# Delta rule on one Trainium2 core: key transposes and M v issued ahead of the triangular inverse, T on M v moved into the recursion, one product table parked in DRAM

## The chip, the cores and the metric

The kernel runs on one core of one Trainium2 chip. The metric is the device time of one execution in microseconds; the time of a kernel is the median of its runs.

## The reference, cut to what matters

Two blocks follow each other on x (256 tokens of width 1024, f32). The first has two hybrid layers, each closed by a feed-forward part (relu, squared). The second joins a differential attention and a delta-rule recursion in two directions, and ends with a mixture of small experts. The change touches the recursion alone:

```python
def wkv_scan(s0, scan_in):
    def step(s, inp):
        w, kk, a, k, v, r = inp
        sa = jnp.einsum('dbhij,dbhj->dbhi', s, kk)
        s = s * w[..., None, :] - sa[..., :, None] * (kk * a)[..., None, :] + v[..., :, None] * k[..., None, :]
        return s, jnp.einsum('dbhij,dbhj->dbhi', s, r)
    return lax.scan(step, s0, scan_in)
...
    s_ctx, y_c = wkv_scan(s0, scan_c)
    _, y_x = wkv_scan(s_ctx, scan_x)
    o_bx = rwkv_post(from_scan(y_x), *aux_x, rw_g_up, rw_r_k, rw_ln_g, rw_ln_b)
```

The scan runs over 256 tokens of the context ("ctx") and then, from the state it leaves, over the 256 tokens of x, with 16 heads of 64 in each of two directions. Of ctx only the last state is used. `rwkv_post` is a mean and a variance per head, a bonus term and a gate.

## The kernel before, in words

Products are f32 made of two parts each, so one linear layer is three matmuls per tile (L333 to L335 with 256 columns, called linA here, and L351 to L353, linB). ACT takes a weight's high part (L312, `wh`), DVE the rest (L277, `wl`).

The recursion is done in chunks of 32 tokens: 8 chunks, which are 8 steps n. The heads are split into two halves `hf` of 8. Thus `wkv_front` and `wkv_back` run four times: ctx's first heads inside the feed-forward part of the first layer, ctx's second heads inside that of the second layer, and x's first and second heads (called x0 and x1) in `second`, beside the projections and the attention. The state goes from ctx to x through DRAM (`Sd`, L906, L1632).

`wkv_front` (L1175) prepares a half's chunks. It loads k, v (and r for x), normalises the keys (L1197, L1206), transposes v and parks it in DRAM (`vtd`), builds the decays and the scaled keys KB and WR, and multiplies them (L1299, "PQ products"); DVE masks the result (L271) into the strictly triangular ML and, for x, the causal products NK. L1314 transposes ML's first half, and `din` carries it through DRAM into Bt. Then comes the inverse T of a unit triangular matrix, 31 pairs of DVE instructions with a width that grows to 256 and falls again (L1328 to L1331, a multiplication by L271 and a subtraction by L277), and back through `dout` with a transpose on DVE (L1338). After it stand in the program: the loads of v (UV) and the transposes of the keys (KT, L1353) and of WR (AT, L1363 for x, L1366 for ctx); M v and then T on M v (one loop over `half`, L1383: 8 calls of 32 matmuls of 32x64 for each half, brought back to UV's rows by ACT, L268); T on W (L1395, called W products) and its scaling by DVE (L271, L1403).

`wkv_back` (L1410) is the recursion. In each step n TensorE multiplies the state (L1429, 32 matmuls, called S>U), DVE adds it to T on M v (L1431, two instructions), TensorE makes the update of the state (L1451, 32 matmuls, K>S) and DVE adds it to the decayed state (L274), which GpSimd made (L1436). For x ACT also copies the step's output out of the bank (L1442, four copies). Each step waits for the one before it. For x a tail follows: NK times U (L1471), mean and variance on DVE (L1476, L1482), the scaling, transposes, the gate (L1497, L1498), ACT (L1501) and the store into `od`.

The instructions' order on each engine is made when the kernel is built: a scheduler runs through the program on modelled times and takes what is ready, with `high_priority(offset=30000)` in favour of the recursion's parts. Buffers decide with it: `w4` and `w8` are pools of 5 and 6 buffers in the feed-forward parts, 8 and 9 in `second`, and a tile waits until its buffer's last reader is done. x1's WR lies in the work tiles `hh` and `hl`, in which the attention's output is written as well, so that this output waits for x1's last S>U. The banks for ctx's products come from two pools in turn (`bank`, L220, stream "c").

The attention over x has 16 iterations, each with two exponentials on ACT (L1533), sums on DVE (L1528), a combination (L1539) and matmuls (L1527, L1550). `od` feeds `merge2`, which follows the recursion of x1.

Of the kernel before, what the change touches and what calls it, by code (L numbers as in the profile page):

```python
# [194 lines left out]
class Kern:  # L195
# [22 lines left out]
        return pool.tile(shape, dtype, tag=tag, name=self.uid(tag), **kw)  # L218

    def bank(self):  # L220
        if self.single == "c":
            self.turn += 1
            return self.t(*((self.psm, [128, 512], "m"), (self.psx, [128, 512], "x"))[self.turn % 2])
        if self.single:
            return self.t(self.psm, [128, 512], "m")
        if not self.sfx and self.spare_bank:
            self.turn += 1
            if self.turn % 3 == 0:
                return self.t(self.psx, [128, 512], "x")
        return self.t(self.psr if self.sfx == "r" else self.psw if self.sfx else self.psa, [128, 512], "a")  # L230
# [657 lines left out]
    def ffn(self, l, pool):  # L888

        nc = self.nc  # L890
        hh = self.t(self.work, [128, 8, T], "hh", F32R)
        hl = self.t(self.work, [128, 8, T], "hl", F32R)
        self.normT(self.halves(self.x), self.P["g_ffn"], hh, hl, spare="t")
        self.mods_units(5, self.last)
        self.spare_bank = False
        if l == 0:
            self.ctx_proj(pool)
        with self.stream("n", "c"), self.tc.high_priority(offset=30000):
            self.n4, self.n8 = 5, 6
            tg = self.t(pool, [128, D], "TG", bufs=4)  # L900
            self.wkv_consts(pool, tg[:, T:T + 264])
            wa = tg[:, :T]
            nc.sync.dma_start(wa, self.wad)
            S = self.t(pool, [128, 2, 4, 64], "S")
            self.wkv_back(pool, self.wkv_front(pool, 0, l, self.zc, wa), S)
            nc.sync.dma_start(self.Sd[l], S)  # L906
        with self.stream("t"):
            pw = [self.bank_pair(), [self.score_bank(), self.score_bank()]]
        prev = None
        for i in range(17):  # L910
            cur = None
# [263 lines left out]
    def wkv_front(self, pool, src, hf, zd, wa, own=False):  # L1175


        nc, C, P = self.nc, self.C, self.P2
# [112 lines left out]
        for q in range(4):  # L1291
# [8 lines left out]
            for b in range(2):  # L1300
                for d in range(2):
                    self.mul(ML[:, d, q, b], pq[b][:, d, :, src], strict[:, 1 - d].unsqueeze(1).to_broadcast([128, 4, 32]))
                    if src:
                        self.mul(NK[:, d, q, b], pq[b][:, d, :, 0], incl[:, d].unsqueeze(1).to_broadcast([128, 4, 32]))

        if src:
            for d in range(2):
# [11 lines left out]
            nc.sync.dma_start(din[c, 0].rearrange("k r s -> r k s"), MT.rearrange("p (k s) -> p k s", s=32)[u])  # L1319
        Bt = self.w4(pool, [128, 32, 32])  # L1320
        nc.sync.dma_start(Bt, din.rearrange("c d k r s -> (c d k) r s"))
        X = self.w4(pool, [128, 32, 32])
        nc.gpsimd.memset(X, 0.0)
        nc.vector.memset(X.rearrange("p a b -> p (a b)")[:, 0::33], -1.0)
# [9 lines left out]
        for c in range(2):  # L1334
# [5 lines left out]
        KT = [k.rearrange("p m (q c) x s -> p m q (c x s)", c=2) for k in KB]  # L1340
        UV = [self.w8(pool, [128, 4, 4, 128]) for e in range(2)]
        for g in range(4):
            rows, at = slice(64 * (g % 2), 64 * (g % 2) + 32), slice(32 * g, 32 * g + 32)
            for t in range(2):
                for d in range(2):
                    n = 4 * t + g if d == 0 else 7 - 4 * t - g
                    nc.sync.dma_start(UV[n % 2][rows, n // 2].rearrange("p m c -> p (m c)"), vtd[at, t])
        for q in range(4):
            for d in range(2):
                qd = q if d == 0 else 3 - q  # L1350
                ps = self.bank().rearrange("p (m c) -> p m c", m=4)
                for m in range(4):
                    nc.tensor.transpose(ps[:, m], KT[d][:, m, qd], self.ident)  # L1353
                self.evac(KT[d][:, :, qd], ps)

        AT = [[self.w4(pool, [128, 2, 4, 128]) for h in range(2)] for d in range(2)]
        for q in range(4):
            for d in range(2):
                at = AT[d][q // 2][:, q % 2]
                ps = self.bank().rearrange("p (m c) -> p m c", m=4)  # L1360
                for m in range(4):
                    if src:
                        nc.tensor.transpose(ps[:, m], WR[d][:, m, 2 * q:2 * q + 2].rearrange("p c x s -> p (c x s)"), self.ident)  # L1363
                        continue
                    for c2 in range(2):
                        mm(ps[64 * c2 + 32:64 * c2 + 64, m], WR[d][:, m, 2 * q + c2, 0], self.ident, start=True, stop=True)  # L1366
                if src:
                    self.evac(at, ps)
                else:
                    for c2 in range(2):  # L1370
                        u = slice(64 * c2 + 32, 64 * c2 + 64)
                        self.evac(at[u], ps[u])
        steps = lambda n: [(d, *divmod(n if d == 0 else 7 - n, 2)) for d in range(2)]
        for half in (0, 32):

            for n in range(8):
                uv = UV[n % 2][:, n // 2]
                ps = self.bank().rearrange("p (m b i) -> p m b i", m=4, b=2)
                for m in range(4):
                    for b in range(2):  # L1380
                        for d, q, c2 in steps(n):
                            R = slice(64 * c2 + half, 64 * c2 + half + 32)
                            mm(ps[64 * c2 + 32:64 * c2 + 64, m, b], ML[R, d, q, b, m], uv[R, m, 64 * b:64 * b + 64], start=True, stop=True)  # L1383
                for c2 in range(2):
                    u = slice(64 * c2 + 32, 64 * c2 + 64)
                    self.evac(uv[u], ps[u].rearrange("p m b i -> p m (b i)"))

        for d in range(2):
            pa = [self.bank().rearrange("p (q m s) -> p q m s", q=4, m=4) for c2 in range(2)]
# [6 lines left out]
            for c2 in range(2):  # L1396
# [6 lines left out]
                    nc.vector.tensor_copy(al[:, first // 2], pa[c2][:, first // 2])  # L1403
                old = PC[:, d, :, 2 * lo + c2 + 2 * d - 1:2 * hi + c2 + 2 * d - 2:2].rearrange("p m q -> p q m")
                self.mul(al[:, lo:hi], pa[c2][:, lo:hi], old.unsqueeze(3).to_broadcast([128, hi - lo, 4, 32]))
        Y = [self.w4(pool, [128, 2, 4, 128]) for d in range(2)] if src else None
        W = [w.rearrange("p m c x s -> p (m c x s)") for w in WR] if src else wc.rearrange("p d m c s -> p (d m c s)")
        return src, hf, PC, W, KT, UV, NK, Y, bond if src else None

    def wkv_back(self, pool, state, S, od=None):  # L1410

        src, hf, PC, W, KT, UV, NK, Y, bond = state
        nc, P = self.nc, self.P2
        mm = nc.tensor.matmul
        m0 = 4 * hf
        U64 = [UV[n % 2][:, n // 2].rearrange("p m (b i) -> p m b i", b=2) for n in range(8)]
        for n in range(8):
            dc = [(d, *divmod(n if d == 0 else 7 - n, 2)) for d in range(2)]
            if src or n:
# [26 lines left out]
            for b in range(2):  # L1446
                Q = slice(64 * b, 64 * b + 64)
                for m in range(4):
                    for d, q, c2 in dc:
                        R = slice(64 * c2, 64 * c2 + 64)  # L1450
                        mm(pk[d][Q, m], KT[d][R, m, q, Q], U64[n][R, m, b], start=True, stop=True)  # L1451
            for d in range(2):
                if n or src:
                    self.add(S[:, d], D[:, d] if n else S[:, d], pk[d])
# [2 lines left out]
        if not src:  # L1457
            for d in range(2):
                self.mul(S[:, d], S[:, d], PC[:, d, :, 7 - 7 * d].unsqueeze(2).to_broadcast([128, 4, 64]))
            return  # L1460

        yf = Y[0]
        for t in range(2):
            ps = self.bank().rearrange("p (m b i) -> p m b i", m=4, b=2)
# [543 lines left out]
```

## Time and profile before

| what | us |
|---|---|
| median of 3 runs | 2866.26 |
| lowest and highest of them | 2864.38 and 2883.52 |
| the profiled execution's own time | 2874.03 |
| its span, first to last instruction | 2872.2 |
| TensorE busy in it | 2672.7 (93%) |
| DVE busy, ACT busy | 1945.2 (68%), 1447.4 (50%) |
| mean granted TensorE clock | 0.949 of 2.4 GHz |

Starts are given in us from the first instruction of the profiled execution. A granted clock of 1.00 in a stretch is 2.4 GHz throughout, 0.50 is 1.2 GHz throughout; between them part of the stretch had the one and part the other. A wait is the idle time of an engine just before an instruction, with the name of what ended it. ctx's first heads lie at 395 to 690, its second heads at 1037 to 1301, x0 at 1397 to 1713 and x1 at 1612 to 1867.

### The profile page before, as it was taken

The page shows a single profiled execution, that of the slowest core. Times are in us where ns is not written, and L with a number is a line of the kernel's source. Part 1 is how long each engine was busy: PE and PEld are TensorE (multiplying, and loading weights), DVE is VectorE, ACT ScalarE, POOL GpSimd, SP SyncE. Part 2 cuts the span into 40 slices and gives each one's busy share as a digit, 9 for nine tenths or more (in the row PEclk, how much of TensorE's full clock was granted, in tenths as well). Part 3 has the DMA queues.
Part 4 walks back from the last instruction along what each step waited for, and adds up shares of the span by engine and source line. Part 5 has one row for each costly group of instructions (what it writes and reads, how often), then busy time and mean ns, then how long its engine had stood idle before and what let it go on. Part 6 is the DMA issues. An engine that isn't in the chain of part 4 may idle for free. (4 is left out here: it accounts for less than half of the span.)

```text
span 2872.2 us, 57632 instructions
## 1 busy us (share of the span) xinstructions
PE 2672.7 (93%) x23136; PEld 2344.7 (82%) x23136; DVE 1945.2 (68%) x3985; ACT 1447.4 (50%) x2440; POOL 57.4 (2%) x112
## 2 busy tenths in 40 slices
PE   7999899999999999987988878888989999999999
PEld 7987598886997768877987755788989998888887
DVE  5986567645797657646787576366887774666665
ACT  4554455643554455634655545445435654444444
POOL 0000000000000000010000010100000000000000
PEclk9999899999999999987999987699999999999999
DMA  5533766545443555524745522055554345666665
GB/s 185 173 126 102 256 216 190 175 133 203 158 155 125 171 176 171 175 83 157 239 144 177 163 66 58 30 192 177 160 184 148 125 145 188 209 215 216 211 215 185
DMA packets 212956, 472.17 MB, mean 164 GB/s; under 512 B 53328, under 2 KB 86992, under 8 KB 211664
## 3 DMA queue, kind: packets, MB, share of 16 engines
q1 hardware_dynamic: 212688, 468.49, 50.6%
q8 instruction: 182, 2.98, 0.4%
q14 instruction: 86, 0.70, 0.1%
HBM read 427.77 MB, written 40.63 MB: 163 GB/s over the span
## 5 line engine op out<-in xcount | busy, mean ns | idle before, releaser
L277 DVE TENSOR_TENSOR wl<-raw,wh 128x1024 fp32r<-128x1024 f32 (+1 forms) x701 | 726.7, 1041 | 415.4 <-ACT wh L312 403.5
L312 ACT ACTIVATE wh<-raw 128x1024 fp32r<-128x1024 f32 (+1 forms) x701 | 637.6, 913 | 686.0 <-PE a L334 225.4
L333 PE MATMUL a<-hh,wh 128*128 128x256 f32 x1928 | 554.1, 288 | 15.2 <-ACT wh L312 7.0
L335 PE MATMUL a<-hh,wl 128*128 128x256 f32 x1928 | 554.5, 288 | 8.8 <-DVE wl L277 8.1
L334 PE MATMUL a<-hl,wh 128*128 128x256 f32 x1928 | 552.5, 287 | 0.6 <-DVE hl L277 0.5
L333 PEld LDWEIGHTS a<-hh,wh 128*128 128x128 f32 x1928 | 371.2, 193 | 25.4 <-ACT wh L312 9.2
L335 PEld LDWEIGHTS a<-hh,wl 128*128 128x128 f32 x1928 | 370.1, 192 | 20.0 <-DVE wl L277 14.5
L334 PEld LDWEIGHTS a<-hl,wh 128*128 128x128 f32 x1928 | 370.7, 192 | 6.5 <-issue 2.3
L335 PE MATMUL x<-hh,wl 128*128 128x256 f32 x712 | 204.0, 287 | 2.9 <-DVE wl L277 2.9
L333 PE MATMUL x<-hh,wh 128*128 128x256 f32 x712 | 202.2, 284 | 3.6 <-ACT wh L312 3.5
L334 PE MATMUL x<-hl,wh 128*128 128x256 f32 x712 | 201.7, 283 | 0.0
L352 PE MATMUL b<-wl,ah 128*128 128x512 f32 x512 | 201.0, 393 | 0.0
L351 PE MATMUL b<-wh,ah 128*128 128x512 f32 x512 | 191.2, 393 | 4.1 <-issue 4.1
L353 PE MATMUL b<-wh,al 128*128 128x512 f32 x512 | 191.7, 391 | 0.0
L333 PEld LDWEIGHTS x<-hh,wh 128*128 128x128 f32 x712 | 134.8, 189 | 6.3 <-ACT wh L312 4.2
L335 PEld LDWEIGHTS x<-hh,wl 128*128 128x128 f32 x712 | 134.4, 189 | 6.6 <-DVE wl L277 5.1
L352 PE MATMUL a<-wl,hh 128*128 128x256 f32 (+2 forms) x400 | 126.6, 317 | 13.8 <-DVE wl L277 13.4
L1857 ACT ACTIVATE ah<-pact 128x256 fp32r<-128x256 f32 x128 | 52.7, 412 | 172.1 <-PE b L352 158.9
L351 PE MATMUL a<-wh,hh 128*128 128x256 f32 (+2 forms) x400 | 122.9, 314 | 16.0 <-ACT wh L312 12.1
L334 PEld LDWEIGHTS x<-hl,wh 128*128 128x128 f32 x712 | 134.3, 189 | 1.4 <-issue 0.8
L277 DVE TENSOR_TENSOR wl<-rawv,wh 128x1024 fp32r<-128x1024 f32 x84 | 101.7, 1222 | 37.9 <-ACT wh L312 37.9
L353 PE MATMUL a<-wh,hl 128*128 128x256 f32 (+2 forms) x400 | 122.9, 309 | 0.0
(704 smaller groups left out, 5606.2 us busy)
## 6 DMA issues: line engine op xcount, KB each, us to landing
raw<-in_flat SPq DMA_DIRECT2D x289, 512.0 KB, 4.0
raw<-in_peer SPq DMA_DIRECT2D x172, 512.0 KB, 4.0
raw<-in_flat SPq DMA_DIRECT2D x228, 256.0 KB, 3.5
rawv<-in_peer SPq DMA_DIRECT2D x84, 512.0 KB, 4.7
TG<-in_flat SPq DMA_DIRECT2D x52, 512.0 KB, 5.9
parked<-act SPq DMA_DIRECT2D x89, 128.0 KB, 2.1
pact<-parked SPq DMA_DIRECT2D x89, 128.0 KB, 4.7
w<-vtd SPq DMA_DIRECT2D x64, 64.0 KB, 2.9
```

The source lines that it names most:

```text
L277: self.nc.vector.tensor_tensor(out, a, b, op=ALU.subtract)
L312: self.nc.scalar.activation(h, src, AF.Copy)
L333: mm(ps, wh[:, k], xh[:, k], start=first and k == 0, stop=False)
L334: mm(ps, wh[:, k], xl[:, k], start=False, stop=False)
L335: mm(ps, wl[:, k], xh[:, k], start=False, stop=last and k == nk - 1)
L351: mm(ps, xh[:, k], wh[:, k], start=first and k == 0, stop=False)
L352: mm(ps, xh[:, k], wl[:, k], start=False, stop=False)
L353: self.last = mm(ps, xl[:, k], wh[:, k], start=False, stop=last and k == nk - 1)
L1857: nc.scalar.activation(ah, act, AF.Copy)
```

## The change

The number of instructions is the same on every engine but SyncE, which gets two DMAs more.

1. In `wkv_front` the loads of v, the transposes KT and AT and M v (`on_values(n, 0)`, 8 calls) stand ahead of the inverse. For ctx, AT's first direction lies in the work tile `xn` instead of a buffer of `w4`.
2. T on M v (`on_values(n, 1)`, 8 calls) is taken out of the loop. For x0 all calls follow the W products. For ctx and x1 a call goes to `wkv_back`: step 0's ahead of the recursion, and that of step n+1 after K>S of step n.
3. x0's NK is written to DRAM (`NKd`) when it is made, and its tail reads it back into a buffer of `w8`.
4. In the second feed-forward part the first 13 banks of stream "c" come from one pool, `psx`.

```diff
@@ bank
+        if self.single == "c" and self.skip:
+            self.skip -= 1
+            return self.t(self.psx, [128, 512], "x")
@@ ffn
+            self.skip = 13 if l else 0
@@ wkv_front, after the PQ products
+        if src and hf == 0:
+            NKd = self.t(self.dram, [128, 2048], "NKd")
+            nc.sync.dma_start(NKd, NK.rearrange("p d q b m s -> p (d q b m s)"))
+            NK = NKd
...
@@ after Bt's load, ahead of X: UV's loads, KT and AT as they stood behind the inverse, and
+        if src:
+            AT = [[self.w4(pool, [128, 2, 4, 128]) for h in range(2)] for d in range(2)]
+        else:
+            xn = self.t(self.xp, [128, 2, 1024], "xn", bufs=1)
+            AT = [[xn[:, h].rearrange("p (q m c) -> p q m c", q=2, m=4) for h in range(2)], [self.w4(pool, [128, 2, 4, 128]) for h in range(2)]]
...
+        def on_values(n, half):
...
+        for n in range(8):
+            on_values(n, 0)
         X = self.w4(pool, [128, 32, 32])
...
@@ behind the inverse, ahead of the W products
-        for half in (0, 32):
-            for n in range(8):
...
@@ behind the W products
+        if src and hf == 0:
+            for n in range(8):
+                on_values(n, 1)
+            on_values = None
@@ wkv_back
+        if on_values:
+            on_values(0, 1)
         for n in range(8):
...
+            if on_values and n < 7:
+                on_values(n + 1, 1)
             for d in range(2):
                 if n or src:
...
+        if hf == 0:
+            NKd, NK = NK, self.w8(pool, [128, 2, 4, 2, 4, 32])
+            nc.sync.dma_start(NK.rearrange("p d q b m s -> p (d q b m s)"), NKd)
```

The lines of the changed kernel are numbered anew: L274 multiplies, L277 adds, L280 subtracts or takes a weight's low part, ACT's L271 brings a bank back; L1452 is the addition to U (before L1431), L1463 the output copies (L1442), L1479 the first state's copy (L1456), L1387 the start of X (L1324).

DVE in the second feed-forward part, at ctx's second heads; `S` is the state, `w8` is U, `wl` a weight's low part and `x_16` the layer's output. Before, in the middle of the recursion:

```order
L274 TENSOR_TENSOR S_1769_11254<-wup_1864_12291,x_1865_12294 128x256
L274 TENSOR_TENSOR S_1769_11254<-wup_1864_12291,m_1866_12295 128x256
L1431 SCALAR_TENSOR_TENSOR w8_1818_11651<-x_1867_12314,urows_1766_11244,w8_1818_11651 128x4x64
L1431 SCALAR_TENSOR_TENSOR w8_1818_11651<-m_1868_12315,urows_1766_11244,w8_1818_11651 128x4x64
L274 TENSOR_TENSOR S_1769_11254<-wup_1869_12334,x_1870_12337 128x256
L274 TENSOR_TENSOR S_1769_11254<-wup_1869_12334,m_1871_12338 128x256
```

and now, at steps 0 and 1:

```order
L1452 SCALAR_TENSOR_TENSOR w8_1814_11576<-m_1854_12155,urows_1765_11243,w8_1814_11576 128x4x64
L280 TENSOR_TENSOR wl_2153_14212<-raw_2151_14209,wh_2152_14211 128x1024
L274 TENSOR_TENSOR mt_2140_14162<-mt_2140_14162 128x512
L280 TENSOR_TENSOR OL_2142_14165<-mt_2140_14162,OT_2141_14164 128x512
L280 TENSOR_TENSOR wl_2156_14218<-raw_2154_14215,wh_2155_14217 128x1024
L1452 SCALAR_TENSOR_TENSOR w8_1814_11576<-x_1855_12156,urows_1765_11243,w8_1814_11576 128x4x64
L277 TENSOR_TENSOR x_16_94<-x_16_94,a_1895_12573 128x512
L277 TENSOR_TENSOR x_16_94<-x_16_94,a_1896_12574 128x512
L277 TENSOR_TENSOR S_1768_11253<-wup_1856_12175,m_1857_12178 128x256
L277 TENSOR_TENSOR S_1768_11253<-wup_1856_12175,x_1858_12179 128x256
```

Before, nothing of the layer stands between the steps; now its linear work reaches into step 1, and only the steps from 2 on stand alone.

DVE at x1's inverse; `w4_2545` is a tile of x0's tail, `w4_2959` (before) and `w4_2989` (now) are X, and `sm`, `dr`, `x_3006` are the attention's. Before, from the last PQ masks to the first pair:

```order
L271 TENSOR_TENSOR w8_2946_19269<-a_2955_19398,consts_5_75 128x128
L271 TENSOR_TENSOR w8_2947_19270<-a_2955_19398,consts_5_75 128x128
L1314 STREAM_TRANSPOSE w4_2956_19441<-w8_2946_19269 128x1024
L274 TENSOR_TENSOR w4_2545_16821<-w4_2545_16821,a_2898_18908 128x512
L1324 MEMSET w4_2959_19450 128x32
L271 TENSOR_TENSOR w4_2960_19453<-w4_2959_19450,w4_2958_19448 128x31
L277 TENSOR_TENSOR w4_2959_19450<-w4_2959_19450,w4_2960_19453 128x31
```

and now, the rows up to the first pair:

```order
L274 TENSOR_TENSOR w4_2545_16822<-w4_2545_16822,a_2907_19080 128x512
L1562 RECIPROCAL dr_3056_20088<-sm_3055_20085 128x2
L1564 SCALAR_TENSOR_TENSOR sm_3057_20090<-sm_3055_20085,dr_3056_20088,nlam_3003_19945 128x1
L1565 SCALAR_TENSOR_TENSOR x_3006_19949<-x_3006_19949,sm_3057_20090 128x512
L1554 TENSOR_REDUCE sm_3064_20110<-x_3062_20108 128x1
L1387 MEMSET w4_2989_19722 128x32
L274 TENSOR_TENSOR w4_2990_19725<-w4_2989_19722,w4_2958_19450 128x31
L280 TENSOR_TENSOR w4_2989_19722<-w4_2989_19722,w4_2990_19725 128x31
```

Before, the tail's mean and all behind it come after the inverse has begun; now the inverse begins after the last DVE instruction of the tail. The buffer of its products `tmp` is one that the tail gives back.

ACT at x1's recursion; `xn_...`, `x_3006`, `junk` and `dt` are the attention's, `w8` is U, `w4` the outputs. Before:

```order
L268 ACTIVATE w8_2964_19526<-a_3000_19928 32x512 x2
L1552 ACTIVATE xn_3012_20097<-a_3197_20636,dr_3189_20609 128x128
L1554 ACTIVATE junk_3198_20642,oss_3013_20098<-xn_3012_20097 128x128
L1575 ACTIVATE xn_3012_20097<-xn_3012_20097,rs_y_3199_20645 128x128 x16
L1442 ACTIVATE w4_3005_20085<-a_3206_20703 32x4x64
L1442 ACTIVATE w4_3006_20086<-a_3206_20703 32x4x64
L1442 ACTIVATE w4_3005_20085<-a_3207_20704 32x4x64
L1442 ACTIVATE w4_3006_20086<-a_3207_20704 32x4x64
```

and now, at a step in the middle:

```order
L271 ACTIVATE w8_2959_19452<-a_3209_20680 32x512 x2
L271 ACTIVATE dt_3161_20401<-a_3160_20396 128x512
L1463 ACTIVATE w4_2997_19935<-a_3210_20701 32x4x64
L1463 ACTIVATE w4_2998_19936<-a_3210_20701 32x4x64
L1463 ACTIVATE w4_2997_19935<-a_3211_20702 32x4x64
L1463 ACTIVATE w4_2998_19936<-a_3211_20702 32x4x64
L1578 ACTIVATE xn_3004_19947<-a_3162_20403,dr_3148_20360 128x128
L1580 ACTIVATE junk_3163_20409,oss_3005_19948<-xn_3004_19947 128x128
L1559 ACTIVATE x_3006_19949,sm_3170_20425<-x_3167_20417,sm_3169_20419 128x512
L1559 ACTIVATE x_3006_19949,sm_3170_20425<-a_3168_20418,sm_3169_20419 128x512
L271 ACTIVATE w8_2960_19453<-a_3215_20746 32x512 x2
```

Before, the 16 scalings of the attention's output stand ahead of the first step; now the steps up to n=4 lie between attention iterations 12 to 16, each with two copies of T on M v ahead of the four output copies, and 5 to 7 come after them.

## Rows read from the trace of the kernel before

**Rows 1.** Windows: us, busy us (instructions) by engine, granted clock, DMA share, GB/s

```profile
1261.00:1301.00 40.00, 29.27 (x522) 25.26 (x515) 19.58 (x62) 2.78 (x6) 8.39 (x14) 0.58 0.07 28
1440.00:1560.00 120.00, 98.36 (x945) 93.37 (x945) 104.44 (x255) 60.56 (x108) 4.74 (x4) 0.93 0.54 163
1560.00:1601.00 41.00, 39.61 (x709) 37.36 (x707) 17.53 (x39) 32.26 (x57) 0.00 (x0) 1.00 0.46 149
1640.00:1715.00 75.00, 59.57 (x954) 43.50 (x952) 53.09 (x112) 42.63 (x99) 13.25 (x14) 0.82 0.28 75
1770.00:1822.00 52.00, 45.73 (x762) 35.98 (x760) 15.57 (x46) 41.00 (x97) 0.00 (x0) 0.86 0.16 51
1822.00:1863.00 41.00, 33.25 (x642) 30.13 (x644) 14.64 (x34) 11.82 (x31) 8.43 (x14) 0.50 0.01 2
```

**Rows 2.** Timeline of DVE, ctx's second heads: start, us, what

```profile
1291.67 0.48 DVE L1431 SCALAR_TENSOR_TENSOR w<-x,urows,w 128x256 f32<-128x256 f32 x1 [1.22 <-PE m L1429]
...
1296.38 0.48 DVE L1431 SCALAR_TENSOR_TENSOR w<-x,urows,w 128x256 f32<-128x256 f32 x1 [1.22 <-PE m L1429]
```

**Rows 3.** Timeline of DVE, additions to U at x1

```profile
1837.58 0.88 DVE L1431 SCALAR_TENSOR_TENSOR w<-a,urows,w 128x256 f32<-128x256 f32 x2 [1.20 <-PE a L1429]
...
1861.74 0.88 DVE L1431 SCALAR_TENSOR_TENSOR w<-a,urows,w 128x256 f32<-128x256 f32 x2 [1.20 <-PE a L1429]
```

**Rows 4.** Timeline of PE, x1's recursion in the granted clock of 0.50

```profile
1838.12 2.57 PE L1451 MATMUL a<-w,w 64*64 64x64 f32 x32 [0.57 <-DVE w L1431]
...
1841.26 0.37 PE L1429 MATMUL a<-S,hl 64*64 64x64 f32 x2 [0.36 <-DVE S L274]
```

**Rows 5.** Timeline of PE, K>S at x0 in the full clock

```profile
1640.59 1.54 PE L1451 MATMUL a<-w,w 64*64 64x64 f32 x32
```

**Rows 6.** Timeline of DVE, x1's inverse, x0's tail in it

```profile
1715.38 0.21 DVE L271 TENSOR_TENSOR w<-w,w 128x31 f32<-128x31 f32 x1 [7.96 <-DMA w<-din]
...
1722.95 1.21 DVE L1476 TENSOR_REDUCE smr<-w 128x16 f32<-128x1024 f32 x1
...
1745.04 0.67 DVE L271 TENSOR_TENSOR w<-w,a 128x512 f32<-128x512 f32 x1
...
1759.96 0.20 DVE L277 TENSOR_TENSOR w<-w,w 128x31 f32<-128x31 f32 x1
...
1768.45 1.24 DVE L1338 STREAM_TRANSPOSE w<-w 32x1024 f32<-32x1024 f32 x1 [0.61 <-DMA w<-dout]
```

**Rows 7.** Timeline of PE, M v among linA in the second feed-forward part

```profile
1203.85 0.28 PE L335 MATMUL a<-hh,wl 128*128 128x256 f32 x1
1203.96 0.28 PE L333 MATMUL a<-hh,wh 128*128 128x256 f32 x1
1204.17 1.08 PE L1383 MATMUL x<-w,w 32*32 32x64 f32 x32
...
1206.42 0.28 PE L333 MATMUL a<-hh,wh 128*128 128x256 f32 x1
...
1206.89 0.28 PE L334 MATMUL a<-hl,wh 128*128 128x256 f32 x1
```

**Rows 8.** Lines of PE, 1560 to 1601, x0: instructions | busy us, mean ns

```profile
L1383 PE MATMUL a<-w,w 32*32 32x64 f32 x512 | 16.0, 215 | 0.9 <-ACT w L268 0.7
```

**Rows 9.** Page, part 6, DMAs of 512 KB: KB each, us to landing

```profile
rawv<-in_peer SPq DMA_DIRECT2D x84, 512.0 KB, 4.7
```

**Rows 10.** Timeline of DVE, x0: T's last transpose, first addition to U

```profile
1560.08 1.24 DVE L1338 STREAM_TRANSPOSE w<-w 32x1024 f32<-32x1024 f32 x1
...
1612.59 0.87 DVE L1431 SCALAR_TENSOR_TENSOR w<-a,urows,w 128x256 f32<-128x256 f32 x2
```

**Rows 11.** Chain of waits at x0: start, us, what

```profile
1601.27 2.13 PE a L1395 x126
```

**Rows 12.** Chain of waits, the attention behind x1's inverse

```profile
1785.88 1.45 ACT x L1533 x4
...
1802.73 1.45 ACT x L1533 x4
```

More of the change, by code (lines that the diff above doesn't have):

```diff
@@ L1321, in wkv_front @@
         nc.sync.dma_start(Bt, din.rearrange("c d k r s -> (c d k) r s"))
+        KT = [k.rearrange("p m (q c) x s -> p m q (c x s)", c=2) for k in KB]
+        UV = [self.w8(pool, [128, 4, 4, 128]) for e in range(2)]
+        for g in range(4):
+            rows, at = slice(64 * (g % 2), 64 * (g % 2) + 32), slice(32 * g, 32 * g + 32)
+            for t in range(2):
+                for d in range(2):
+                    n = 4 * t + g if d == 0 else 7 - 4 * t - g
+                    nc.sync.dma_start(UV[n % 2][rows, n // 2].rearrange("p m c -> p (m c)"), vtd[at, t])
@@ new lines, in wkv_front @@
+        for q in range(4):
+            for d in range(2):
+                qd = q if d == 0 else 3 - q
+                ps = self.bank().rearrange("p (m c) -> p m c", m=4)
+                for m in range(4):
+                    nc.tensor.transpose(ps[:, m], KT[d][:, m, qd], self.ident)
+                self.evac(KT[d][:, :, qd], ps)
+        if src:
[3 more added lines that the diff above has]
+            AT = [[xn[:, h].rearrange("p (q m c) -> p q m c", q=2, m=4) for h in range(2)], [self.w4(pool, [128, 2, 4, 128]) for h in range(2)]]
@@ new lines, in wkv_front @@
+        for q in range(4):
+            for d in range(2):
+                at = AT[d][q // 2][:, q % 2]
+                ps = self.bank().rearrange("p (m c) -> p m c", m=4)
+                for m in range(4):
+                    if src:
+                        nc.tensor.transpose(ps[:, m], WR[d][:, m, 2 * q:2 * q + 2].rearrange("p c x s -> p (c x s)"), self.ident)
+                        continue
+                    for c2 in range(2):
+                        mm(ps[64 * c2 + 32:64 * c2 + 64, m], WR[d][:, m, 2 * q + c2, 0], self.ident, start=True, stop=True)
+                if src:
+                    self.evac(at, ps)
+                else:
+                    for c2 in range(2):
+                        u = slice(64 * c2 + 32, 64 * c2 + 64)
+                        self.evac(at[u], ps[u])
@@ new lines, in wkv_front @@
+        steps = lambda n: [(d, *divmod(n if d == 0 else 7 - n, 2)) for d in range(2)]
+        def on_values(n, half):
+            uv = UV[n % 2][:, n // 2]
+            ps = self.bank().rearrange("p (m b i) -> p m b i", m=4, b=2)
+            for m in range(4):
+                for b in range(2):
+                    for d, q, c2 in steps(n):
+                        R = slice(64 * c2 + 32 * half, 64 * c2 + 32 * half + 32)
+                        mm(ps[64 * c2 + 32:64 * c2 + 64, m, b], ML[R, d, q, b, m], uv[R, m, 64 * b:64 * b + 64], start=True, stop=True)
+            for c2 in range(2):
+                u = slice(64 * c2 + 32, 64 * c2 + 64)
+                self.evac(uv[u], ps[u].rearrange("p m b i -> p m (b i)"))
@@ L1338, in wkv_front @@
             nc.vector.transpose(ML[:, 1].rearrange("p q b m s -> p (q b m s)")[u], TB[u].rearrange("p k s -> p (k s)"))
[L1340 to L1372, printed above, removed]
@@ L1373, in wkv_front @@
-        steps = lambda n: [(d, *divmod(n if d == 0 else 7 - n, 2)) for d in range(2)]
-        for half in (0, 32):
-            for n in range(8):
[L1377 to L1386, printed above, removed]
@@ L1405, in wkv_front @@
                 self.mul(al[:, lo:hi], pa[c2][:, lo:hi], old.unsqueeze(3).to_broadcast([128, hi - lo, 4, 32]))
+        if src and hf == 0:
+            for n in range(8):
+                on_values(n, 1)
+            on_values = None
         Y = [self.w4(pool, [128, 2, 4, 128]) for d in range(2)] if src else None
         W = [w.rearrange("p m c x s -> p (m c x s)") for w in WR] if src else wc.rearrange("p d m c s -> p (d m c s)")
-        return src, hf, PC, W, KT, UV, NK, Y, bond if src else None
+        return src, hf, PC, W, KT, UV, on_values, NK, Y, bond if src else None
     def wkv_back(self, pool, state, S, od=None):
-        src, hf, PC, W, KT, UV, NK, Y, bond = state
+        src, hf, PC, W, KT, UV, on_values, NK, Y, bond = state
         nc, P = self.nc, self.P2
```

## The prediction, made before the run

> **What bounds the kernel now.** I read the windows first. TensorE is busy nearly all the time, so what it doesn't do costs nothing; a change of order pays only where it stands. Four places bear on this change [rows 1]. At ctx's second heads (1261 to 1301) it is busy for 29.27 of 40 us at a granted clock of 0.58. At x0's inverse (1440 to 1560) it stands for 120 - 98.36 = 21.6 us, and DVE, busy for 104.44, is what it waits for. From 1560 to 1601 it is full (39.61 of 41). From 1640 on it has gaps again, and in x1's recursion (1822 to 1863) it is busy for 33.25 of 41 us at a clock of 0.50, with nothing else on any engine: DMA moves 2 GB/s there.
>
> The timelines say what these two bare recursions are: chains. Two additions to U follow each other at 1291.67 and 1296.38, 4.71 us apart, each waiting for S>U [rows 2]; x1's are 1837.58 and, five steps on, 1861.74, 4.83 us apart [rows 3]. Of a step K>S takes 2.57 us at this clock [rows 4], where it took 1.54 in the full one [rows 5]. Ahead of x1's recursion the chain runs through x1's inverse on DVE, from 1715.38 to 1759.96, with x0's tail (its mean at 1722.95, its last product at 1745.04) between its instructions [rows 6], and then through the attention with M v between its matmuls.
>
> **The change part by part.** I give each part's effect on the profiled execution (2874.03 us); the median of the runs is 7.8 us below it, and I take that off at the end.
>
> *A. ctx's first heads: 0, between -2 and +2.* In both orders their steps lie among the linear layers of the first feed-forward part. The same matmuls are done in the same full stretch; the bounds are two calls of M v at 1.08 us [rows 7] either way.
>
> *B. ctx's second heads: -4, between -12 and +6.* Eight calls of M v leave the path ahead of the bare part; one takes 1.08 us [rows 7], 8.6 together, and linear work now covers steps 0 and 1. Left bare are six steps instead of eight, and each has a call of T on M v between K>S and S>U. At half clock that call would be about twice 1.08; it hides the 0.36 us in which S>U waits for the sum of S [rows 4], so I estimate 4.71 + 1.9 - 0.4 = 6.2 a step. Six are 37 us, eight were 38. So the bare stretch stays as long, and the gain is what had room in the full one: half of the 8.6, as linear work is drawn in there. The lower price of a step is 4.71, if ACT's copies and the call hide wholly (-9 more); the upper is 8.3, where the two copies, the call and the wait all follow each other (+12, against which stands the 8.6).
>
> *C. x0's front: W products 24 us earlier.* In 1560 to 1601 TensorE does 512 matmuls of M v and T on M v [rows 8], 16 calls at 1.08 or 17.3 us, and about 104 matmuls of linA that now stand behind the first W products; they start 0.117 us apart (1206.42 to 1206.89, four of them [rows 7]), so 12.2 us. The 8 calls of half 0 and the transposes go into the 21.6 us idle of 1440 to 1560, which hides them; if ACT, busy half that time, were late with the copies, 8.6 us would come back. Against it, x0's T is later. 19 more DVE instructions stand ahead of the last transpose of T, at 104.44 / 255 = 0.41 us or 8 us in all. And Bt's load waits on SyncE behind NK's way back, which waits for the write: 512 KB take 4.7 us to land [rows 9], NK has 1 MB, so 4.7 to 9.4, and I take 6. That is 14 us. T was there at 1560.08 + 1.24 = 1561 [rows 10], so it is now at 1575. The first W products started at 1601.27 [rows 11]; TensorE would be free for them at 1601.3 - 29.5 = 1572, so T decides, and they start at 1577: 24 us earlier.
>
> *D. x0's recursion and x1's front: 5 us longer.* It gets the 12.2 us of linA and 8.6 of T on M v, and gives three of five attention iterations back to later; one takes 8.4 us where it has two calls of M v in it [rows 12], and I count 4 us of TensorE for it, 12 in all. That is +8.8; the 75 - 59.57 = 15.4 us in which TensorE stands in 1640 to 1715 take some of it, and I count 5. So x0's tail comes 24 - 5 = 19 us earlier, and its mean on DVE at 1723 - 19 = 1704 [rows 6].
>
> *E. x1: the inverse behind the tail.* The `tmp` buffer now comes from x0's tail, so that the inverse can't begin until the tail is through. The tail took 23 us from its mean to its last product, with the inverse's instructions in between [rows 6]. Its DVE work in that is about 9 us (four instructions like the 1.21 us mean, five like the 0.67 us product, and small ones), and with the turns over ACT and TensorE I take 11 alone. The inverse starts at 1704 + 11 = 1715, as before. But it is shorter now: it took 44.6 us, and without the tail's 9 leaves 36. The way to the last transpose stays 1769.7 - 1760.1 = 9.6 us [rows 6]. From the first W products to the first addition to U x0 took 11.3 us (1601.27 to 1612.59) [rows 10, 11], so 12 here. Before, x1 had all 16 calls ahead of this place, 17.3 us at full clock, among attention iterations of (1802.73 - 1785.88) / 2 = 8.4 us [rows 12], with 16 pairs of copies on ACT, which was busy for 41 of 52 us [rows 1]. Now step 0 comes at 1715 + 36 + 9.6 + 12 = 1773. Four steps go along with four attention iterations, which bound them: 4 x 8.4 = 34. Three are bare at 6.2 as in B: 18.6. The last addition to U is at 1825 instead of 1861.74, 36 us earlier, and all that waits for it (the attention's output in x1's buffers, the merge) moves with it. The steps' own price has bounds: 4.83 and 8.3 in the bare ones (-4, +6), and 6 to 10 in the joint ones (-10, +6).
>
> The sum is 0 - 4 - 36 = -40: 2834 in the profiled execution, 2826 as a median.
>
> A rule bears on B and E. In [rows 7] a step from linA to M v's small matmuls takes 0.21 us to the next start instead of 0.11, and the trace shows no more. The Trainium skill, TensorEngine Tiling (Array Packing), Key Properties, says that a change of the tiling mode empties TensorE first. T on M v works on 32 rows between products of 64; by that rule each bare step has two more such changes, and at 0.1 us each that would be 0.2 us a step, under 2 us in all nine.
>
> **The rivals.**
>
> *R1, no room gained, within 1%: 2846.* x0's tail doesn't come earlier: what W gains, the linA moved behind it, T on M v and waits in x0's recursion take away again. For it: x0's recursion has waits on DVE and ACT as much as on TensorE (53.09 and 42.63 of 75 us [rows 1]), so less TensorE work ahead needn't shorten it. Against it: 15 us idle there. The inverse would start at 1734, the last addition be at 1844 (-18), and with B at -2: -20, 2854, or 2846 as a median.
>
> *R2, slower: 2876.* The serial lock decides. x1's inverse needs 36 + 9.6 + 12 + 34 + 18.6 = 110 us to the last addition, so a start later than 1861.74 - 110 = 1752 turns the gain into a loss. It would come if x0's tail were drawn out behind the attention's work on ACT and DVE, and the bare steps took 8.3. With the start at 1752 x1 gives 0, the three steps at 8.3 give +6 and B +6, less 2: 2884, or 2876. For it: the tail turns several times between DVE, ACT and TensorE, each time behind attention work in the queues. Against it: it took 23 us even among the inverse's instructions.
>
> *R3, the clock: 2807.* The bare stretches stand at 0.50 and 0.58 [rows 1], that is at 1.2 GHz for most of them. The calls now fill some of their waits. If the clock goes to 2.4 GHz there, K>S takes 1.54 instead of 2.57 [rows 4, 5], and a step with all of it about 4.0 instead of 6.2: nine steps give 19 us more. For it: in 1640 to 1715, where x0's steps lie among other work with waits of their own, the clock was 0.82 [rows 1]. Against it: it stayed at 0.50 through all of x1's steps. The Trainium skill, TensorE: Matmul & The Clock Gate, Part 1, says that the slow clock is the default and activity releases it; that speaks for R3, and by it the sum would be the 2807 above.
>
> **How the numbers follow.** My forecast has 0.58, R1 0.24, R3 0.11, R2 0.07. The likeliest is 2826. Its own range, by the bounds in B, C and E, is 2806 to 2846. To hold eight times in ten it takes in R1 with its spread and most of R3: 2796 to 2860. About 1%, 29 us, is what a measurement of this kernel can tell from no change, so faster is under 2838 and slower over 2895. The forecast lies under 2838 in some 0.50 of its 0.58, R3 wholly: 0.61. R2 over 2895 in less than half, with mishaps that I don't see: 0.05. The rest, 0.34, is within 1%.
>
> **What would show it.** Right: x0's W products at about 1577 and its tail's mean at 1704; x1's inverse beginning at about 1715 and lasting 36 us without the tail's instructions; additions to U at 8.4 us in the joint steps and 6.2 in three bare ones at a clock of 0.50; the last at 1825; ctx's bare steps six in number. Wrong: an inverse that begins after 1730 (R1), or after 1752 (R2); a clock near 1.00 in the bare stretches (R3); and W products that don't come earlier at all, for then C has failed.

## The result, and the profile after

The changed kernel takes 2838.74 us in the median of 4 runs (2832.16 to 2842.35), the kernel before 2867.96 in 4 runs on the same chip: a ratio of 0.9887, interval 0.9851 to 0.9923. Its profiled execution took 2832.16 us (span 2830.3). On another chip the ratio was 0.9905 (0.9873 to 0.9937).

Three of the windows of [rows 1], with the same limits, in the changed kernel, and two more in x1's recursion:

```profile
1261.00:1301.00 40.00, 27.94 (x432) 25.19 (x428) 9.52 (x28) 5.07 (x9) 5.52 (x16) 0.50 0.11 32
1440.00:1560.00 120.00, 105.02 (x1209) 101.38 (x1204) 103.96 (x261) 68.93 (x120) 4.73 (x4) 0.93 0.57 181
1790.00:1803.60 13.60, 13.15 (x223) 9.64 (x222) 8.93 (x23) 10.74 (x28) 2.90 (x4) 1.00 0.13 42
1803.60:1814.50 10.90, 9.13 (x211) 8.09 (x210) 5.71 (x20) 7.36 (x19) 2.40 (x4) 1.00 0.37 123
1822.00:1863.00 41.00, 37.82 (x537) 36.18 (x532) 30.61 (x54) 20.27 (x35) 2.12 (x1) 0.88 0.56 175
```

At x0's inverse TensorE now works 105.0 of 120 us (98.4 before), and the last window holds the merge at 175 GB/s where it held the bare recursion at 2 GB/s. DVE's timeline at the places of [rows 3, 6, 10], x0's first, then x1's:

```profile
1566.03 1.24 DVE L1401 STREAM_TRANSPOSE w<-w 32x1024 f32<-32x1024 f32 x1
...
1578.90 0.88 DVE L1452 SCALAR_TENSOR_TENSOR w<-a,urows,w 128x256 f32<-128x256 f32 x2 [2.25 <-PE a L1450]
...
1679.79 1.22 DVE L1502 TENSOR_REDUCE smr<-w 128x16 f32<-128x1024 f32 x1
...
1704.01 0.09 DVE L1387 MEMSET w<- 128x32 f32 x1
...
1741.42 0.21 DVE L280 TENSOR_TENSOR w<-w,w 128x31 f32<-128x31 f32 x1
...
1750.88 1.24 DVE L1401 STREAM_TRANSPOSE w<-w 32x1024 f32<-32x1024 f32 x1 [0.25 <-DMA w<-dout]
...
1769.99 0.88 DVE L1452 SCALAR_TENSOR_TENSOR w<-a,urows,w 128x256 f32<-128x256 f32 x2 [0.35 <-PE a L1450]
...
1803.56 0.86 DVE L1452 SCALAR_TENSOR_TENSOR w<-a,urows,w 128x256 f32<-128x256 f32 x2
...
1824.13 0.88 DVE L1452 SCALAR_TENSOR_TENSOR w<-a,urows,w 128x256 f32<-128x256 f32 x2 [3.63 <-ACT w L271]
```

x0's first addition to U came 34 us earlier (1578.9, 1612.6 before), x0's mean 43 (1679.8, 1723.0), x1's recursion began 58 us earlier (1770.0, 1828.0 before) and its last addition came 37.6 earlier (1824.1, 1861.7): it now runs among the attention, at 54 us for 34. All that follows keeps the 38 us and wins 4 more. Of these times 6.7 us lie ahead of x0: ctx's state is ready at 1293.1, and was at 1299.8.

### The profile page after: what moved, and what is told of

Its sections match the earlier page's. It is cut to its first block, busy times and chain, and to the rows that moved or that the text cites. A ratio compares the mean times of both kernels' runs of the same rounds, so it can differ in the third digit from the quotient of the medians.

```text
span 2830.3 us, 57640 instructions
## 1 busy us (share of the span) xinstructions
PE 2675.2 (95%) x23136; PEld 2344.7 (83%) x23136; DVE 1953.1 (69%) x3985; ACT 1447.6 (51%) x2440; POOL 61.0 (2%) x112
## 4 chain that ended last, share of the span: by engine, by line
PE 80%; DVE 9%; DMA 5%; ACT 4%; issue 2%; SPq 0%; DVEq 0%; ACTq 0%
PE a L338 8%; PE a L336 8%; PE a L337 8%; PE b L356 4%; PE b L354 4%; PE b L355 4%; PE b L1848 3%; PE a L355 3%; PE a L354 3%; PE a L356 3%; PE x L338 3%; PE x L337 3%; PE x L336 3%; DVE wl L280 3%; DMA raw<-in_peer 2%
## 5 line engine op out<-in xcount | busy, mean ns | idle before, releaser
L280 DVE TENSOR_TENSOR wl<-raw,wh 128x1024 fp32r<-128x1024 f32 (+1 forms) x701 | 728.6, 1043 | 403.1 <-ACT wh L315 390.4
L336 PEld LDWEIGHTS a<-hh,wh 128*128 128x128 f32 x1960 | 370.6, 189 | 19.1 <-ACT wh L315 11.5
L336 PE MATMUL x<-hh,wh 128*128 128x256 f32 x680 | 195.1, 287 | 5.8 <-ACT hh L1702 2.9
L337 PE MATMUL x<-hl,wh 128*128 128x256 f32 x680 | 195.3, 287 | 2.2 <-DVE hl L280 1.7
L338 PE MATMUL x<-hh,wl 128*128 128x256 f32 x680 | 194.6, 286 | 2.5 <-DVE wl L280 2.4
L354 PE MATMUL a<-wh,hh 128*128 128x256 f32 (+2 forms) x416 | 126.7, 311 | 15.3 <-DMA raw<-in_flat 11.4
L355 PE MATMUL a<-wl,hh 128*128 128x256 f32 (+2 forms) x416 | 130.3, 313 | 11.1 <-DVE wl L280 10.9
L280 DVE TENSOR_TENSOR wl<-rawv,wh 128x1024 fp32r<-128x1024 f32 x84 | 101.7, 1222 | 37.8 <-ACT wh L315 37.6
```

The source lines that it names most:

```text
L280: self.nc.vector.tensor_tensor(out, a, b, op=ALU.subtract)
L336: mm(ps, wh[:, k], xh[:, k], start=first and k == 0, stop=False)
L337: mm(ps, wh[:, k], xl[:, k], start=False, stop=False)
L338: mm(ps, wl[:, k], xh[:, k], start=False, stop=last and k == nk - 1)
L354: mm(ps, xh[:, k], wh[:, k], start=first and k == 0, stop=False)
L355: mm(ps, xh[:, k], wl[:, k], start=False, stop=False)
```

## The experiments

Ratios are to the kernel before on the same chip. To compare profiles of different chips, the table counts from the moment at which ctx's state is ready (its last scaling on DVE, 1299.8 before and 1293.1 after); "clock" is the granted clock of the stretch from x1's first to its last addition to U. The times are of one profiled execution each: those of changed, changed_again, plain, plain_again and nk_stays were the fastest of their runs, those of split_copy and no_skip the slowest.

| kernel | ratio | x0's first addition | x1's first | x1's last | recursion of x1 | clock |
|---|---|---|---|---|---|---|
| before | 1 | 312.8 | 528.2 | 562.0 | 33.8 | 0.50 |
| behind_inverse | 1.0016 (0.9991 to 1.0041) | 306.2 | 513.6 | 555.6 | 42.0 | 0.62 |
| at_alone | 0.9956 (0.9934 to 0.9978) | 291.6 | 508.6 | 553.9 | 45.3 | 0.65 |
| no_skip | 0.9921 (0.9894 to 0.9949) | 289.7 | 498.1 | 551.4 | 53.3 | 0.69 |
| two_ahead | 0.9969 (0.9945 to 0.9992) | 290.4 | 475.6 | 550.2 | 74.6 | 0.63 |
| ctx2_ahead | 0.9947 (0.9928 to 0.9965) | 288.8 | 469.9 | 549.1 | 79.1 | 0.59 |
| split_copy | 0.9932 (0.9912 to 0.9951) | 286.8 | 473.5 | 538.4 | 64.9 | 0.68 |
| x1_ahead | 0.9920 (0.9900 to 0.9940) | 283.7 | 471.5 | 532.2 | 60.7 | 0.70 |
| all_ahead | 0.9889 (0.9855 to 0.9923) | 289.3 | 474.5 | 533.9 | 59.4 | 0.71 |
| plain_again | 0.9890 (0.9848 to 0.9931) | 287.9 | 473.7 | 531.9 | 58.2 | 0.74 |
| changed_again | 0.9905 (0.9873 to 0.9937) | 288.3 | 477.3 | 531.4 | 54.2 | 0.81 |
| changed | 0.9887 (0.9851 to 0.9923) | 285.8 | 476.9 | 531.0 | 54.1 | 0.82 |
| nk_stays | 0.9901 (0.9870 to 0.9932) | 288.1 | 477.0 | 526.0 | 49.0 | 0.92 |
| plain | 0.9898 (0.9869 to 0.9928) | 289.9 | 470.4 | 517.0 | 46.6 | 1.00 |

**Which part carries the gain.** behind_inverse takes the changed kernel and puts the block from UV's loads to M v behind the inverse again; as a diff, the inverse goes ahead of it:

```diff
         nc.sync.dma_start(Bt, din.rearrange("c d k r s -> (c d k) r s"))
+        X = self.w4(pool, [128, 32, 32])
...
+            nc.vector.transpose(ML[:, 1].rearrange("p q b m s -> p (q b m s)")[u], TB[u].rearrange("p k s -> p (k s)"))
...
         for n in range(8):
             on_values(n, 0)
-        X = self.w4(pool, [128, 32, 32])
...
```

> KT, AT and M v stand behind the inverse again, as before the change; T on M v stays where the change put it, and so do NK's way through DRAM and the banks. Theory (the place ahead of the inverse carries the gain): x0's first W products are 8 us earlier than before at most, x1's recursion starts after 1800 with all eight steps bare at 6 to 7 us, its last addition to U comes at 1855 to 1870, and the time is 2860 (2850 to 2872). Rival (moving T on M v carries it): the last addition to U stays under 1835 and the time under 2846.

The gain was gone (2875.78 us, 1.0016), the theory's side, though 4 us over its range; x1's last addition came at 1869.5, inside it. at_alone starts from the kernel before and moves AT's four buffers and its transposes alone:

```diff
+        if src:
+            AT = [[self.w4(pool, [128, 2, 4, 128]) for h in range(2)] for d in range(2)]
...
         X = self.w4(pool, [128, 32, 32])
```

> The kernel before with one block moved: AT (its four buffers and the eight groups of transposes of WR) stands ahead of the inverse, for x alone; KT, M v, T on M v, NK and the banks stay as before the change. Theory (AT's buffers, claimed behind X and tmp in the program, held AT back until the inverse was through, and M v stood behind AT for the banks): this block alone carries x's gain. x0's first addition to U comes 280 to 292 us after ctx's state is ready (313 before, 286 in the changed kernel), x1's last 522 to 545 after it (562 before, 531 changed), ctx as before, time 2843 (2834 to 2853). Rival (M v's place or T on M v in the steps is needed too): the last addition stays 550 us or more behind ctx's state, time 2858 or more.

Half each, and the time lies between (2852.94 us, 0.9956). x0's first addition came at 291.6, as the theory said, 21 of the changed kernel's 27 us, so AT's block is what held x0. This run moves the buffers and the transposes together; for the buffers, claimed behind those of X and tmp, speaks the trace of the kernel before. KT's transposes, which stand behind the inverse there as well but need no new buffer, ran at 1484 to 1494, ahead of its first pair at 1495.8. Of AT's eight groups TensorE made two right behind them, as many as this stream has banks. ACT's copies of these two into AT's buffers came only after the inverse, whose last subtraction ended at 1549.8, and the other six groups after those (TensorE's and ACT's timelines):

```profile
1497.20 0.60 PE L1363 MATMUL a<-ident,w 128*128 128x128 f32 x4
...
1552.35 1.08 ACT L268 ACTIVATE w<-a 128x512 f32<-128x512 f32 x2
...
1555.07 1.04 PE L1363 MATMUL a<-ident,w 128*128 128x128 f32 x8
```

But x1's last came at 553.9, the rival's side. TensorE's timeline in at_alone shows why; T's last transpose ends at 1748.8:

```profile
1749.18 1.91 PE L1402 MATMUL a<-w,w 32*32 32x64 f32 x30
...
1759.75 3.63 PE L1402 MATMUL a<-w,w 32*32 32x64 f32 x64
...
1773.91 1.92 PE L1402 MATMUL a<-w,w 32*32 32x64 f32 x32
...
1777.77 4.93 PE L1414 MATMUL a<-w,w 32*64 32x32 f32 x128
```

T on M v (L1402), in the program ahead of the W products (L1414), keeps them from 1749 to 1778, with the attention's products between its calls; M v itself (the same line) was through at 1735.5. x1's first addition comes 47.7 us after the start of T's last transpose (460.9 to 508.6), against 19.1 in the changed kernel (457.8 to 476.9), both at a clock of 0.50. So the second half of the gain is T on M v standing behind W. This is read from the traces; no run moves it alone onto at_alone. Where behind W it stands is what the next three ask.

**In the steps or ahead of them.** The condition under which all eight calls are issued behind W, ahead of the recursion, for ctx2_ahead, x1_ahead and all_ahead in this order:

```diff
-        if src and hf == 0:
+        if (src == 0) == (hf == 1):
+        if src:
+        if True:
             for n in range(8):
                 on_values(n, 1)
```

> For x1 all eight calls of T on M v stand ahead of the recursion; ctx keeps them in its steps. Theory: x1's joint steps are bound by the attention iterations (8.4 us), so calls taken out of them save little there, and the bare steps fall to 4.8; the recursion begins some 9 us later than at 1770 and ends at 1820 to 1830, as now at 1824. Time 2839 (2832 to 2847). Rival (the move into the steps carries the gain of x1): the last addition to U comes 15 us later, at 1840 or after, and the time is 2854 or more.

> All eight calls of T on M v stand ahead of the recursion in all four places: of the change, only the transposes, M v ahead of the inverse, NK's way and the banks are left. Theory (the place ahead of the inverse carries the gain, the move into the steps little): ctx as in the run with ctx's calls ahead (bare steps 4.7, state 2 to 3 us earlier against its T), x1's recursion begins some 8 us later than the changed kernel's and ends between its 1824 and 15 us later, by the clock that it gets; time 2848 (2836 to 2860). Rival (the move into the steps carries half of the gain or more): the last addition to U comes 18 us later or more, time 2858 or more.

> For ctx's second heads all eight calls of T on M v stand ahead of the recursion, behind the W products; the rest is the changed kernel. Theory (two banks): a bare step of ctx takes 7.1 us in the changed kernel, since a call waits for a bank, and S>U's second half for the same bank, which ACT's two copies give back; without the call a step is back at 4.7 us (before: 4.71), six or seven bare steps, and the front pays 8 x 1.08 = 8.6 us at full clock. The state is ready 0 to 6 us earlier than the changed kernel's 1293, and the time is 2834 (2826 to 2842). Rival (the call one step ahead is what gained 7 us there): the state is ready at about 1300 as before the change, and the time is 2846.

x1_ahead and all_ahead came out at 2847.29 (0.3 over the theory's range) and 2836.91, on the theory's side: x1's first addition comes 16.3 and 17.9 us after the start of T's last transpose, and all_ahead without any call in a step is as fast as the changed kernel. ctx2_ahead did at ctx what the theory said; its steps there are 4.70 us apart:

```profile
1270.21 0.48 DVE L1452 SCALAR_TENSOR_TENSOR w<-m,urows,w 128x256 f32<-128x256 f32 x1 [1.22 <-PE x L1450]
...
1274.91 0.48 DVE L1452 SCALAR_TENSOR_TENSOR w<-m,urows,w 128x256 f32<-128x256 f32 x1 [1.23 <-PE x L1450]
```

and yet it took 2857.9 us, over the theory's range: the time was lost 500 us later, at x1, where the scheduler gave another order as well and the clock stayed low.

**The clock at x1.** two_ahead, whose order at x1 is that of ctx2_ahead:

```diff
             on_values(0, 1)
+            on_values(1, 1)
...
-            if on_values and n < 7:
-                on_values(n + 1, 1)
+            if on_values and n < 6:
+                on_values(n + 2, 1)
```

> T on M v is issued two steps ahead in the recursion instead of one; all else is the changed kernel. Its order at x1 is that of the run with ctx's calls ahead: both W products first, then one step to each attention iteration up to n=6. Theory (the order at x1 sets the clock, and the clock the time): x1's recursion takes 70 to 80 us from the first to the last addition to U, as in that run (79), not 54, at a granted clock of 0.5 to 0.65, the bare steps of ctx stay at 7.1, since the banks bind them, and the time is 2855 (2846 to 2865). Rival (the 79 us came of ctx's calls or of chance, and the copies of T on M v lie on the chain at x1): the recursion takes 48 to 54 us, its last step under 7 instead of 9.6, and the time is 2834 or less.

The theory held: 2862.8 us, 74.6 us of recursion at a clock of 0.63. The mean clocks of the ten runs of two_ahead and the ten of ctx2_ahead, 0.941 to 0.949, speak against a chance of the one profiled. plain has all calls ahead and no NKd; plain_again and changed_again repeat plain and the changed kernel.

> The changed kernel with T on M v ahead of every recursion and NK left in its buffer: of the change only the place of KT, AT and M v, ctx's AT in xn and the 13 banks are left. Theory (the rest of the change gives nothing that counts): as the run with all calls ahead, 2838 (2830 to 2848). Rival (the way of NK through DRAM or the calls in the steps carry some of it): 2850 or more.

> The kernel of the run named plain, unchanged, once more. Its ten runs lay between 2815.5 and 2855.6 us, with a mean granted clock between 0.963 and 0.945. Theory (the clock granted in x1's recursion is what differs from one execution of a program to the next): in this profile too the time from x1's first to its last addition to U follows the clock in it, 47 us at 1.00, 54 at 0.8, 60 at 0.7, 75 or more under 0.65, and over the runs the time falls as the mean clock rises, about 20 us for 0.01. Rival (the spread comes of DMA or of the first blocks): the recursion takes 46 to 49 us at any clock, and time and mean clock are not ordered alike.

> The changed kernel itself once more, on this chip. Theory (x1's recursion takes the clock that it is granted, whatever the order): the time from x1's first to its last addition to U lies on the line of the other runs, 49 us at a clock of 0.92, 54 at 0.82, 60 at 0.70, whatever clock it gets here; time 2838 (2830 to 2848). Rival (the order alone sets it): 53 to 55 us at any clock.

They took 2831.95, 2836.31 and 2833.49 us, inside the ranges given for plain and changed_again. changed_again got a clock of 0.81, the changed kernel's within a hundredth, and the same 54 us, so it doesn't part its theory from its rival; plain_again does. The windows of plain and of plain_again, one program, from x1's first to its last addition to U:

```profile
1750.80:1797.50 46.70, 42.33 (x735) 31.11 (x734) 25.90 (x63) 32.12 (x83) 10.24 (x14) 1.00 0.12 39
```

```profile
1754.80:1813.00 58.20, 54.92 (x734) 41.13 (x734) 26.07 (x61) 32.57 (x83) 10.25 (x14) 0.74 0.10 31
```

DVE and ACT worked the same 26 and 32 us in both; TensorE's clock was 1.00 and 0.74, and the recursion took 46.6 and 58.2. Recursion times clock is 42 to 47 us in the ten profiles of the table from two_ahead down (the rows above them have less of the attention in the stretch): TensorE binds this stretch and its clock sets the time. plain's ten runs fit this for the whole: 2815.5 us at a mean clock of 0.963, 2843 at 0.951, 2855.6 at 0.945. What lifts the clock in one execution and not in the next, and why the order of two_ahead and ctx2_ahead leaves it at 0.6, these runs don't show.

**The smaller parts.** NK left in its buffer, without the write and the read (nk_stays); one of two copies by DVE (split_copy); and stream c's banks in turn from the start (no_skip):

```diff
-            NKd = self.t(self.dram, [128, 2048], "NKd")
-            nc.sync.dma_start(NKd, NK.rearrange("p d q b m s -> p (d q b m s)"))
...
+                if half and c2:
+                    nc.vector.tensor_copy(uv[u], ps[u].rearrange("p m b i -> p m (b i)"))
...
-            self.skip = 13 if l else 0
+            self.skip = 0
```

> NK of x0 stays in its buffer; the write to DRAM and the read back are gone, the rest is the changed kernel. Theory (the way through DRAM costs nothing that counts): x0's inverse may begin up to 5 us earlier, since Bt's load stands behind the read, but DVE is full there, and x1's inverse begins within 5 us of 1704; time 2837 (2829 to 2846). Rival (it holds up x0's inverse): x0's first addition to U and all that follows come 5 us earlier or more, time 2832 or less. Second rival (it frees the buffer that x1's front needs): x1's PQ products come 8 us later or more, time 2848 or more.

> Of the two copies that bring T on M v back, one is done by DVE instead of ACT, in all four recursions; all else is the changed kernel. Theory (ACT's two copies of 0.6 us, one after the other, are part of a bare step): ctx's bare steps fall from 7.1 to 6.5, ctx's state is ready 3 to 4 us earlier against its T, x1's last steps gain 1 to 3 us, and the time is 2834 (2826 to 2842). Rival (TensorE at half clock binds the step and the copies are hidden): the step stays at 7.1 and the time at 2838 or above.

> The first 13 banks of the second feed-forward part come from both pools in turn again; all else is the changed kernel. ctx's bare steps are five, and at x1 two steps lie among the attention and six are bare. Theory (the banks' turn matters by the order alone): ctx within 4 us of the changed kernel; x1's six bare steps at 6 to 7 us take as long as there joint ones, so that the recursion takes 52 to 60 us; time 2842 (2834 to 2852). Rival (the pool's choice carries part of the gain at ctx): ctx's state is ready 6 us later or more against its T, time 2850 or more.

nk_stays is the changed kernel within the interval (2844.83 us, 0.9901): NK's way costs nothing and frees nothing that counts. split_copy (2848.55) settles little: DVE's copy began only when ACT's had ended, so the two did not run side by side, and the step stayed at 7.2 us, where the rival put it:

```profile
1282.95 0.70 DVE L1382 COPY w<-m 32x512 f32<-32x512 f32 x1 [2.31 <-ACT w L271]
```

no_skip took 2846.9 us, inside the theory's range. Its x1 recursion took 53.3 us, as expected, but began at 498.1, 21 us after the changed kernel's; its interval overlaps the changed kernel's, and whether the 13 banks matter stays open.

## Why the prediction was right, step by step

The profiled execution was forecast at 2834 and took 2832.16; x1's last addition at 1825, and it came at 1824.1. That these two meet so well is luck. 1825 was counted from x0's T in the profile before and left out B's 4 us; counted from ctx's state, the last addition came 30.9 us earlier for my 36. The 6.7 us up to ctx's state and 4.3 after x1, for my 4 and 0, make up the sum. The median was forecast at 2826 and is 2838.74, inside the range. The term that failed there is the shift: I took 7.8 us off because the profile of before lay above its median, and the profile of after lies 6.6 below its own. With plain's 40 us from run to run, by the clock, a profile is no nearer to the median than that.

A was not measured by itself. B's size is not resolved: ctx's state came 6.7 us earlier for my 4, but the same instructions reach it at 1299.8 in the profile before and at 1286.6 in at_alone's, and the changed kernel's at 1293.1 and, in changed_again, at 1297.9. What is resolved are the steps: six bare ones, as forecast, but 7.1 us apart (1276.02 to 1283.12) and not 6.2. The timeline of TensorE shows the wrong idea, that the call hides S>U's wait:

```profile
1271.65 1.92 PE L1378 MATMUL x<-w,w 32*32 32x64 f32 x32 [0.58 <-DVE S L277]
1273.50 1.12 PE L1450 MATMUL m<-S,w 64*64 64x64 f32 x16
1274.86 1.12 PE L1450 MATMUL x<-S,w 64*64 64x64 f32 x16 [0.24 <-ACT w L271]
```

ctx's stream has one bank of each name, m and x. The call needs x, which the sum of S is still reading, and S>U's second half waits for x until ACT has made both copies. So the call's 1.92 us at 1.2 GHz, and part of the copies, add to the 4.71 in full; ctx2_ahead, without it, has 4.70. The clock was 0.50 as forecast.

C: the W products of x0 began at 1563.6, all but 18 of them from 1565.5 on, for my 1577, and x0's first addition came 34 us earlier, 27 of them counted from ctx's state. The sum of T's delay was right, its parts were not: counted from ctx's state T came 12.6 us later (260.3, then 272.9) for my 14, but NK's way has no share in it, since nk_stays has T at 275.7. 11.4 us of it lie ahead of the inverse's first pair (196.1, then 207.5), so it arose ahead of the inverse and not in it. That linA stands aside and M v goes into TensorE's gaps was right: 256 matmuls of L1378, T on M v alone, remain in 1560 to 1601, where [rows 8] has 512.

D was wrong in sign: from x0's first addition to its mean 100.9 us, 110.4 before. I priced the three attention iterations that went out at 4 us of TensorE each, and the 8.4 us that one takes [rows 12] is nearer: 12.2 + 8.6 - 25.2 = -4.4; the rest is not resolved.

E: the inverse began at 1704, 11 us earlier than forecast, as the sum of two errors: the mean 24 us earlier (1679.8 for 1704), the tail 24 us long and not 11, as its turns stand behind three attention iterations on DVE. My reason for the tail going first, the buffer of tmp, is not shown: X's buffer was cleared by GpSimd at 1680.86 and Bt's load issued at 1680.79, so these two did not hold the inverse until 1704. Whether tmp's buffer did, or only DVE's order, made on modelled times, the trace can't say, as it names no buffers, and no run tried it. After that the terms hold in their sums: the inverse 37.6 us for 36, to the last transpose 10.5 for 9.6, four joint steps 33.6 for 34 (1770.0 to 1803.6), three behind them 20.6 for 18.6. Only T to the first addition took 18 for 12: TensorE was busy for all of 1750.9 to 1770, at a clock of 0.50. The steps themselves were not what I forecast. The joint ones are 11.1, 8.8, 6.9 and 6.8 us apart, not 8.4 each, and the three behind them 6.4, 4.6 and 9.6, not 6.2 each at 0.50. That their sums came out is luck too: in nk_stays, with the same steps at a clock of 1.00, the four joint ones took 27.9.

The last step, of 9.6 us at a clock of 0.69, was not bare. ACT's timeline:

```profile
1814.53 4.78 ACT L1601 ACTIVATE xn<-xn,rs_y 128x128 f32<-128x128 f32 x16
...
1822.91 1.19 ACT L271 ACTIVATE w<-a 32x512 f32<-32x512 f32 x2 [2.04 <-PE a L1378]
```

The attention's 16 scalings went between, and TensorE's transposes of their results between K>S's matmuls.

Of the rivals R1 and R2 did not come. R3 came in part: not in the bare steps of ctx (0.50), but at x1, where the clock was 0.50 in the first joint step and 1.00 from 1790 to 1814.5. That takes in the last two joint steps, where I had not put it, and two of the three behind them, where I had named it as a sign of being wrong. The Trainium skill's rule on tiling modes (TensorEngine Tiling (Array Packing), Key Properties) leaves no mark that these runs can resolve.

## What to carry to other kernels

A block can hold a chain by where it claims its buffers or by what it stands ahead of: AT's buffers, claimed behind the inverse's, held back x0, and T on M v, written ahead of the W products, held back x1. Find what stands first behind the long wait and put only what the chain needs there; whether the rest then goes into the steps or ahead of them was worth nothing here. And before a variant is read by its time alone, read the granted clock of the stretch it changed: 46.6 and 58.2 us were one program. Then look whether a forecast that came true did so term by term: here two sums met by terms that erred both ways.

## What was not expected of the hardware

One and the same program got clocks of 0.74 and 1.00 in the same stretch in two executions (on two chips), and its ten runs on one chip lay between 2815.5 and 2855.6 us, by and large the longer the lower their mean clock. Two orders with one step to each attention iteration stayed at 0.59 and 0.63 there, and took 20 to 30 us more than the same work at 0.8 or more. Nor does a busy TensorE by itself bring the full clock: in at_alone it was busy for all of 47.7 us from 1747.5 to 1795.2, and the granted clock was 0.50 throughout.
